# A second copy of the scan state, and its scaled copy made earlier, in an encoder layer

## The chip, the cores and the metric

The kernel runs on one core of a Trainium2 chip. The metric is the device time of one execution in microseconds (us); lower is better. A core has five engines with a queue of instructions each: PE (matmuls, with the loading of weights shown apart as PEld), DVE (elementwise work), ACT (elementwise work and functions), POOL (elementwise work) and SP (here it only issues DMAs). Each engine takes its instructions in the order of the program; between engines they wait on semaphores.

## The reference

One encoder layer over two sequences, of 512 and 1024 tokens, with 1024 features. It has a feed-forward part, then a mixer, then a second feed-forward part. Half of the mixer is a linear recurrence (`wkv_scan`), run forwards and backwards over 8 heads of 64 features:

```python
def step(S, inp):
    r_t, w_t, k_t, v_t, na_t, b_t = inp
    sa = jnp.einsum('bhvk,bhk->bhv', S, na_t)
    S = S * w_t[:, :, None, :] + sa[..., None] * b_t[:, :, None, :] + v_t[..., None] * k_t[:, :, None, :]
    y = jnp.einsum('bhvk,bhk->bhv', S, r_t)
    return S, y
...
m = jnp.concatenate([pool_mixer(...), rwkv7_mixer(...)], axis=-1)
m = m.astype(x.dtype) @ w_out
```

S is a 64 x 64 matrix for each head and direction, zero at the start. All values are float32.

## The kernel before

The kernel works on three blocks of 512 tokens (two of the long sequence, one of the short one). The feed-forward parts and projections are long runs of dense matmuls: 128x128 weights on 512 columns, each product in three matmuls (high x high, high x low, low x high halves of the values; tiles `hh`, `hl`, `gh`, `gl` and weights `whi`, `wlo`). They write PSUM tiles named `u`, `v` and `y`. There are 11556 of them.

The recurrence is computed in chunks of L = 64 tokens. Two heads go together, so there are four pairs of heads for each sequence. A "macro" is 8 chunks (two groups `gi` of 4 chunks `c`), with both directions `d` side by side; 12 macros make 96 chunks. `scan_prep` makes a group's operands (AR, BKt, MU), `scan_inv` inverts its triangular matrices by columns on DVE or POOL, `scan_state` runs through the chunks in order, and `scan_post` normalises the result. The projection `wout_gen` of a block waits for the result of `scan_post`.

A chunk of `scan_state` has three steps, each ended by a `yield WAIT`:

1. **W**: matmuls (lines 1366 and 1369) multiply the old state SBD by AR, and MA by part of UV, into the direction's PSUM bank, columns 0 to 127; ACT copies W to `iw` (line 1371; the profile calls its tile XN).
2. **U**: matmuls (line 1375) into columns 128 to 255 of the bank; ACT copies U into UV (line 1377; the profile calls its tile MU). Then ACT makes `s0p`, the old state scaled by the decay of the chunk (line 1381).
3. **Update and output**: matmuls of line 1386 put the state's increment into columns 0 to 63; lines 1391 (reads the old state) and 1393 put the chunk's output into 64 columns from 256 on. DVE then writes the new state over the old one: increment x decay + `s0p` (lines 1399 and 1401), in four instructions: two directions by two heads.

The last chunk of a pair of heads makes no update, and the first has no old state. The 8 PSUM banks include one for each direction, `bank[d]`, which holds W, U, the increment and the output of four chunks.

The order of all instructions is made while the program is built. `run_until` keeps a set of processes (the dense stream, the four scan processes, norms) and emits the next piece of the ready one with the best priority. Whether one is ready is decided by `Estimate`, a table of costs: it keeps a time at which each engine is free, and for each region of a tile when it was last written and read. After `yield WAIT` the state's process is ready again 200 ns after the estimated end of everything that its step issued; until then dense matmuls are emitted. `Estimate` compares regions of the state's bank by address. The waits themselves are not from this table; they are added afterwards from what each instruction reads and writes.

Of the kernel before, what the change touches and what calls it, by code (L numbers as in the profile page):

```python
# [12 lines left out]
AF = mybir.ActivationFunctionType  # L13
ALU = mybir.AluOpType
# [3 lines left out]
P = 128  # L18
# [5 lines left out]
L = 64  # L24
# [140 lines left out]
def rev(ap):  # L165
    a = [list(x) for x in ap.ap]
    st, n = a[-1]
    a[-1] = [-st, n]
    return bass.AP(tensor=ap.tensor, offset=ap.offset + st * (n - 1), ap=a)
# [3 lines left out]
def encoder_kernel(ctx, tc, x_prompt, x_sample, c_prompt, c_sample, ada_w, ada_b, n1_pre, n1_post,  # L173
# [5 lines left out]
    V, S, G, T, SY = (Queue(est, *q) for q in (("V", nc.vector), ("S", nc.scalar), ("G", nc.gpsimd), ("T", nc.tensor),  # L179
                                               ("Y", nc.sync)))  # L180
# [3 lines left out]
    def nm(s):  # L184
        uid[0] += 1
        return f"{s}{uid[0]}"
# [15 lines left out]
    def mt(shape, tag, bufs, dt=F32, pool=None):  # L202
        return est.ring((pool or mp).tile(shape, dt, name=nm(tag), tag=tag, bufs=bufs), (id(pool), tag), bufs)
# [4 lines left out]
    class Proc:  # L208
        def __init__(self, gen, prio):
            self.gen, self.prio, self.ready, self.cond = gen, prio, est.free["T"], None  # L210
# [67 lines left out]
    def has(*k):  # L278
        return lambda: all(x in flags for x in k)

    def mm(out, lhsT, rhs, start=True, stop=True):
        T.matmul(out, lhsT, rhs, start=start, stop=stop, skip_group_check=True)
# [853 lines left out]
    class ScanBufs:  # L1136
        def __init__(self, sp):
            self.sp = sp
            f = lambda shape, n: sp.tile(shape, F32, name=nm(n), tag=n, bufs=1)
            self.AR = f([P, 2, 2, 4, 2, L], "AR")  # L1140
            self.BKt = f([P, 2, 2, 4, P], "BKt")
            self.MU = f([P, 3, 32, L], "MU")
            self.MA, self.MR = self.MU[:, 0], self.MU[:, 1]
            self.UV = self.MU[:, 2].rearrange("p (g d c h) f -> p g d c h f", g=2, d=2, c=4)
            self.XN = f([P, 61, 32], "XN")
            self.iw = self.XN[0:64, 53:61, :].rearrange("p t s -> p (t s)")
            self.SBD = f([P, 2, P], "SBD")
            self.Pt = f([P, 2, 4, L + 1], "Pt")
            self.PL = f([P, 2, 2, 2, 4], "PL")
            self.bank = [ps.tile([P, TB], F32, name=nm("sb"), tag=f"s{d}", bufs=1) for d in range(2)]  # L1150
            G.memset(self.SBD, 0.0)
            G.memset(self.Pt, 1.0)
            self.yT, self.bq = {}, {}

# [2 lines left out]
    def st_(sb, shape, tag, bufs=1):  # L1157
        return mt(shape, tag, bufs, pool=sb.sp)
# [183 lines left out]
    def scan_state(sb):  # L1342


        AR, BKt, UV, MA, MR, SBD, PL = sb.AR, sb.BKt, sb.UV, sb.MA, sb.MR, sb.SBD, sb.PL
        both = range(2)
        half = [slice(64 * h, 64 * h + 64) for h in both]
        Wp = [sb.bank[d][half[d], 0:P] for d in both]
        Up = [sb.bank[d][half[d], P:2 * P] for d in both]
        hl_ = lambda h: slice(h * L, (h + 1) * L)  # L1350
        for m, (i_, hf) in enumerate(macros):
            g, p = pairs[i_]
            nblk = GT[g] // GL
            nh = nblk // 2
            for c8 in range(8):
                gi, c = c8 // 4, c8 % 4
                if c == 0:
                    yield has(("inv", m, gi))
                zero = hf == 0 and c8 == 0
                lastc = hf == nh - 1 and c8 == 7  # L1360
                us = lambda d, h: gi * 16 + d * 8 + h * 4 + c
                wsb = [sb.iw[:, d * P:(d + 1) * P] for d in both]
                s0p = {}
                if not zero:
                    for d in both:
                        mm(Wp[d], AR[:, gi, d, c, 0, :], SBD[:, d, :], stop=False)
                for h in both:
                    for d in both:
                        mm(Wp[d][:, hl_(h)], MA[64:128, us(d, h), :], UV[64:128, gi, d, c, h, :], start=zero)
                for d in both:  # L1370
                    S.activation(wsb[d], Wp[d], AF.Copy)
                yield WAIT
                for h in both:
                    for d in both:
                        mm(Up[d][:, hl_(h)], MA[0:64, us(d, h), :], wsb[d][:, hl_(h)])
                for d in both:
                    S.activation(UV[0:64, gi, d, c].rearrange("p h f -> p (h f)"), Up[d], AF.Copy)
                if not zero and not lastc:
                    for d in both:
                        s0p[d] = st_(sb, [P, P], f"s0p{d}")  # L1380
                        S.activation(s0p[d], SBD[:, d, :], AF.Copy, scale=PL[:, m % 2, gi, d, c:c + 1])
                yield WAIT
                if not lastc:
                    for d in both:
                        for h in both:
                            mm(sb.bank[d][half[h], 0:L], BKt[:, gi, d, c, half[h]], UV[:, gi, d, c, h, :])
                yo = slice(256 + c * L, 256 + c * L + L)
                for d in both:
                    if not zero:
                        for h in both:  # L1390
                            mm(sb.bank[d][half[h], yo], SBD[half[h], d, half[h]], AR[half[h], gi, d, c, 1, :], stop=False)
                    for h in both:
                        mm(sb.bank[d][half[h], yo], UV[:, gi, d, c, h, :], MR[:, us(d, h), :], start=zero)
                if not lastc:
                    for d in both:
                        for h in both:
                            pl_ = PL[half[h], m % 2, gi, d, c:c + 1]
                            if zero:
                                V.tensor_scalar(SBD[half[h], d, half[h]], sb.bank[d][half[h], 0:L], pl_, None, op0=ALU.mult)
                            else:  # L1400
                                V.scalar_tensor_tensor(SBD[half[h], d, half[h]], sb.bank[d][half[h], 0:L], pl_,
                                                       s0p[d][half[h], half[h]], ALU.mult, ALU.add)
                if c == 3:
                    t = 2 * hf + gi
                    if t == 0:
                        if i_ >= 1:
                            yield has(("post", i_ - 1))
                        sb.yT[i_] = st_(sb, [P, GT[g]], "yT")
                    for d in both:
                        gb = t if d == 0 else nblk - 1 - t  # L1410
                        o = sb.yT[i_][:, gb * GL:(gb + 1) * GL]
                        if d == 1:
                            o = rev(o)
                        if t >= nh:
                            V.tensor_tensor(o, o, sb.bank[d][:, 256:512], ALU.add)
                        else:
                            S.activation(o, sb.bank[d][:, 256:512], AF.Copy)
                        flags.add(("st", m, gi, d))
                yield WAIT
# [183 lines left out]
    with tc.tile_pool(name="late", bufs=1, reuse_waits="tile") as lp:  # L1603
        sb = ScanBufs(lp)
        scanning.append(sb)

        spawn(scan_state(sb), 0)
        spawn(scan_inv(sb, 0), PRIO_INV)
        spawn(scan_inv(sb, 1), PRIO_INV)
        spawn(scan_prep(sb), PRIO_PREP)  # L1610
        spawn(scan_post(sb), PRIO_POST)

        run_until(has(("m", 1), ("m", 0)))
        scanning.clear()
# [35 lines left out]
```

## Time and profile before

| | |
|---|---|
| timed runs, us | 3717.42, 3724.97, 3725.17 (median 3724.97) |
| profiled execution, us | 3731.42, with a span of 3729.7 |
| mean granted clock of PE | 0.948 |
| matmuls into the scan's bank (sb) | first at about 1265 us, last at about 2660 us |
| s0p on ACT | 160 instructions, mean 392 ns |
| writes of the state on DVE | 352 instructions, median 284 ns |

The profile lists instructions by tiles, as out<-in, with buffer numbers left out; x4 behind a row says that four were merged. All instructions carry the line of one helper (L161), so that rows are told apart by their tiles. `sb<-SBD,AR` is the part of W with the old state, `sb<-XN,MU` is U, `sb<-MU,BKt` is the increment, `sb<-AR,SBD` and `sb<-MU` behind it are the output, and `SBD<-sb,PL,s0p` is the update. A value in brackets is the engine's idle time just before the row, with what ended it.

### The profile page before, as it was taken

To read this page: it belongs to the slowest core of one execution; us is meant where nothing else is said; L and a number is where in the kernel's file an instruction comes from. 1 tells how busy PE (TensorE), PEld (TensorE's weight loads), DVE (VectorE), ACT (ScalarE), POOL (GpSimd) and SP (SyncE) were. 2 spreads that over 40 slices of the span, in tenths; PEclk is the share of its full clock that TensorE was granted. 3 is DMA by queue.
4 is the path that set the end of the run, shared out by engine and by line. 5 is a ranking of instruction groups with operands and counts; after the bars stand their busy time and mean duration, and the time that the engine had idled before them with its cause. 6 is when DMAs were issued, how large, how long until landed. Compare 5 with 4: busy or idle time off the path is not lost. (4 is left out here: it accounts for less than half of the span.)

```text
span 3729.7 us, 53665 instructions
## 1 busy us (share of the span) xinstructions
PE 3511.1 (94%) x19579; PEld 2656.5 (71%) x19579; DVE 2014.5 (54%) x3817; ACT 1443.7 (39%) x2778; POOL 1399.6 (38%) x1700
## 2 busy tenths in 40 slices
PE   7999999998999999999889978899999999999998
PEld 4667878886676676776656656667787788877886
DVE  3128262227227878787877687777557522242223
ACT  3324252224335444444444434444334432233222
POOL 2333444443232322233414324432354344444444
PEclk8999999998999998999979978799999999999999
DMA  7655343334344322222423343222354333334332
GB/s 277 226 183 180 92 150 99 90 99 122 123 123 141 91 66 89 74 83 83 138 79 105 111 147 119 69 85 64 99 181 130 111 109 90 100 117 121 95 92 79
DMA packets 557980, 432.11 MB, mean 116 GB/s; under 512 B 27029, under 2 KB 511572, under 8 KB 553620
## 3 DMA queue, kind: packets, MB, share of 16 engines
q1 hardware_dynamic: 524900, 379.90, 33.2%
q10 hardware_dynamic: 32816, 48.78, 4.1%
q8 instruction: 155, 2.54, 0.3%
q14 instruction: 109, 0.89, 0.1%
HBM read 367.23 MB, written 61.34 MB: 115 GB/s over the span
## 5 line engine op out<-in xcount | busy, mean ns | idle before, releaser
L161 POOL TENSOR_TENSOR wlo<-wraw,whi 128x512 fp32r<-128x512 f32 x666 | 884.9, 1347 | 1288.3 <-ACT whi L161 819.6
L161 DVE TENSOR_TENSOR y<-y,y 128x512 f32<-128x512 f32 x480 | 328.1, 685 | 879.9 <-PE y L161 878.8
L161 ACT ACTIVATE whi<-wraw 128x512 fp32r<-128x512 f32 x938 | 559.4, 622 | 184.8 <-PE v L161 141.3
L161 PE MATMUL u<-hl,whi 128*128 128x512 f32 x1392 | 568.4, 408 | 19.5 <-DVE hl L161 18.4
L161 PE MATMUL u<-hh,whi 128*128 128x512 f32 x1392 | 568.9, 409 | 15.8 <-ACT hh L161 4.2
L161 PE MATMUL v<-hh,whi 128*128 128x512 f32 x1392 | 566.5, 407 | 11.6 <-ACT hh L161 6.2
L161 PE MATMUL v<-hl,whi 128*128 128x512 f32 x1392 | 565.9, 407 | 8.3 <-DVE hl L161 8.3
L161 PE MATMUL u<-hh,wlo 128*128 128x512 f32 x1392 | 570.7, 410 | 0.1
L161 PE MATMUL v<-hh,wlo 128*128 128x512 f32 x1392 | 565.1, 406 | 0.0
L161 PE MATMUL y<-gh,whi 128*128 128x512 f32 x1056 | 424.8, 402 | 9.9 <-DVE y L161 8.2
L161 PE MATMUL y<-gh,wlo 128*128 128x512 f32 x1056 | 423.8, 401 | 2.5 <-DVE wlo L161 2.5
L161 PE MATMUL y<-gl,whi 128*128 128x512 f32 x1056 | 422.4, 400 | 0.0
L161 POOL TENSOR_TENSOR XN<-XN 64x126 f32<-64x126 f32 (+22 forms) x744 | 331.2, 445 | 177.3 <-DVE XN L161 60.7
L161 ACT ACTIVATE gh<-s 128x512 fp32r<-128x512 f32 x132 | 83.5, 632 | 644.9 <-DVE s L161 644.9
L161 PEld LDWEIGHTS u<-hl,whi 128*128 128x128 f32 x1392 | 268.3, 193 | 88.7 <-DVE hl L161 24.8
L161 PEld LDWEIGHTS u<-hh,whi 128*128 128x128 f32 x1392 | 268.6, 193 | 86.5 <-ACT hh L161 7.9
L161 PEld LDWEIGHTS v<-hh,whi 128*128 128x128 f32 x1392 | 266.9, 192 | 80.7 <-ACT hh L161 9.7
L161 PEld LDWEIGHTS v<-hl,whi 128*128 128x128 f32 x1392 | 267.0, 192 | 75.7 <-DVE hl L161 12.5
L161 PEld LDWEIGHTS u<-hh,wlo 128*128 128x128 f32 x1392 | 268.4, 193 | 70.2 <-issue 10.2
L161 PEld LDWEIGHTS v<-hh,wlo 128*128 128x128 f32 x1392 | 267.4, 192 | 64.7 <-issue 7.2
L161 PEld LDWEIGHTS y<-gh,whi 128*128 128x128 f32 x1056 | 200.5, 190 | 63.9 <-DVE y L161 11.6
L161 PEld LDWEIGHTS y<-gh,wlo 128*128 128x128 f32 x1056 | 200.8, 190 | 51.3 <-DVE wlo L161 3.7
(252 smaller groups left out, 4322.6 us busy)
## 6 DMA issues: line engine op xcount, KB each, us to landing
wraw<-in_f_w_dram SPq DMA_DIRECT2D x792, 256.0 KB
ada<-in_ada_w_dram SPq DMA_DIRECT2D x32, 1024.0 KB
wraw<-in_w_in_dram SPq DMA_DIRECT2D x98, 256.0 KB
xk<-xs ACTq DMA_DIRECT2D x96, 256.0 KB
xs<-y ACTq DMA_DIRECT2D x48, 256.0 KB
wraw<-in_w_out_dram SPq DMA_DIRECT2D x48, 256.0 KB
in_k<-zk SPq DMA_DIRECT2D x48, 128.0 KB
in_kk<-zkk SPq DMA_DIRECT2D x48, 128.0 KB
```

Source lines behind the costliest of these rows:

```text
L161: return f(*args, **kw)
```

## The change

There are two copies of the state, and chunks take turns: chunk `c8` reads copy `c8 % 2` and writes the other. Both are set to zero once, since only their diagonal blocks are written later. And `s0p` is made in step 1, after the copies of W, instead of in step 2, after the copies of U.

```diff
-            self.SBD = f([P, 2, P], "SBD")
+            self.SBD = [f([P, 2, P], "SBD%d" % i) for i in range(2)]
...
-            G.memset(self.SBD, 0.0)
+            for t in self.SBD:
+                G.memset(t, 0.0)
...
+                old, new = SBD[c8 % 2], SBD[1 - c8 % 2]
                 if not zero:
                     for d in both:
-                        mm(Wp[d], AR[:, gi, d, c, 0, :], SBD[:, d, :], stop=False)
+                        mm(Wp[d], AR[:, gi, d, c, 0, :], old[:, d, :], stop=False)
...
                 for d in both:
                     S.activation(wsb[d], Wp[d], AF.Copy)
+                if not zero and not lastc:
+                    for d in both:
+                        s0p[d] = st_(sb, [P, P], f"s0p{d}")
+                        S.activation(s0p[d], old[:, d, :], AF.Copy, scale=PL[:, m % 2, gi, d, c:c + 1])
                 yield WAIT
...
                 for d in both:
                     S.activation(UV[0:64, gi, d, c].rearrange("p h f -> p (h f)"), Up[d], AF.Copy)
-                if not zero and not lastc:
-                    for d in both:
-                        s0p[d] = st_(sb, [P, P], f"s0p{d}")
-                        S.activation(s0p[d], SBD[:, d, :], AF.Copy, scale=PL[:, m % 2, gi, d, c:c + 1])
                 yield WAIT
...
-                            mm(sb.bank[d][half[h], yo], SBD[half[h], d, half[h]], AR[half[h], gi, d, c, 1, :], stop=False)
+                            mm(sb.bank[d][half[h], yo], old[half[h], d, half[h]], AR[half[h], gi, d, c, 1, :], stop=False)
...
-                                V.scalar_tensor_tensor(SBD[half[h], d, half[h]], sb.bank[d][half[h], 0:L], pl_,
+                                V.scalar_tensor_tensor(new[half[h], d, half[h]], sb.bank[d][half[h], 0:L], pl_,
                                                        s0p[d][half[h], half[h]], ALU.mult, ALU.add)
```

Line 1399, the update of a first chunk, changes in the same way. Since `Estimate` sees other tiles and another order on ACT, the order of the whole program behind the scan's start changes. Three places show how. The numbers behind the names only tell buffers apart.

On ACT, one chunk of the second macro before: the copies of W (XN), then of U (MU), then s0p for both directions.

```order
L161 ACTIVATE XN_9076<-sb_9080 64x128
L161 ACTIVATE XN_9076<-sb_9081 64x128
L161 ACTIVATE MU_9075<-sb_9080 64x128
L161 ACTIVATE MU_9075<-sb_9081 64x128
L161 ACTIVATE s0p_11118<-SBD_9077,PL_9079 128x128
L161 ACTIVATE s0p_11120<-SBD_9077,PL_9079 128x128
```

The same chunk on ACT now:

```order
L161 ACTIVATE XN_9076<-sb_9081 64x128
L161 ACTIVATE XN_9076<-sb_9082 64x128
L161 ACTIVATE s0p_11109<-SBD_9078,PL_9080 128x128
L161 ACTIVATE s0p_11111<-SBD_9078,PL_9080 128x128
L161 ACTIVATE MU_9075<-sb_9081 64x128
L161 ACTIVATE MU_9075<-sb_9082 64x128
```

The two s0p instructions moved ahead of the copies of U, and read the copy of the state whose turn it is.

On PE, in the same macro, from the last matmul of W to the first of U, before (rows with 128x512 are dense matmuls):

```order
L161 MATMUL sb_9081<-MU_9075 64x64
L161 MATMUL u_10964<-hl_8857,whi_10885 128x512
L161 MATMUL u_10964<-hh_8856,wlo_10960 128x512
L161 MATMUL y_11109<-gh_10417,whi_10871 128x512
L161 MATMUL y_11109<-gl_10418,whi_10871 128x512
L161 MATMUL sb_9080<-XN_9076,MU_9075 64x64
```

And the same piece of PE now:

```order
L161 MATMUL sb_9082<-MU_9075 64x64
L161 MATMUL u_10966<-hl_8857,whi_10887 128x512
L161 MATMUL u_10966<-hh_8856,wlo_10962 128x512
L161 MATMUL y_11121<-gh_10423,whi_10873 128x512
L161 MATMUL y_11121<-gl_10424,whi_10873 128x512
L161 MATMUL y_11121<-gh_10423,wlo_10889 128x512
L161 MATMUL y_11121<-gh_10689,whi_10873 128x512
L161 MATMUL y_11121<-gl_10690,whi_10873 128x512
L161 MATMUL y_11121<-gh_10689,wlo_10889 128x512
L161 MATMUL sb_9081<-XN_9076,MU_9075 64x64
```

Four more dense matmuls stand between W and U; in the same chunk four fewer, 4 for 8, stand between U and the increment.

On PE, from that chunk's output to the W of the next chunk, before:

```order
L161 MATMUL sb_9081<-AR_9073,SBD_9077 64x64 x2
L161 MATMUL sb_9081<-MU_9075 64x64 x2
L161 MATMUL v_11140<-hl_8729,whi_10958 128x512
L161 MATMUL v_11140<-hh_8728,wlo_11003 128x512
L161 MATMUL v_11140<-hh_8728,whi_10958 128x512
L161 MATMUL sb_9080<-SBD_9077,AR_9073 64x128
```

And now:

```order
L161 MATMUL sb_9082<-AR_9073,SBD_9078 64x64 x2
L161 MATMUL sb_9082<-MU_9075 64x64 x2
L161 MATMUL v_11148<-hl_8729,whi_10960 128x512
L161 MATMUL v_11148<-hh_8728,wlo_11005 128x512
L161 MATMUL sb_9081<-SBD_9077,AR_9073 64x128
```

One dense matmul fewer stands ahead of the matmul that needs the new state.

More of the change, by code (lines that the diff above doesn't have):

```diff
@@ L1398, in scan_state @@
                             if zero:
-                                V.tensor_scalar(SBD[half[h], d, half[h]], sb.bank[d][half[h], 0:L], pl_, None, op0=ALU.mult)
+                                V.tensor_scalar(new[half[h], d, half[h]], sb.bank[d][half[h], 0:L], pl_, None, op0=ALU.mult)
                             else:
-                                V.scalar_tensor_tensor(SBD[half[h], d, half[h]], sb.bank[d][half[h], 0:L], pl_,
+                                V.scalar_tensor_tensor(new[half[h], d, half[h]], sb.bank[d][half[h], 0:L], pl_,
                                                        s0p[d][half[h], half[h]], ALU.mult, ALU.add)
```

## The prediction

> **What bounds the kernel now.** I read the page first, for the engine that is always busy.
>
> ```profile
> span 3729.7 us, 53665 instructions
> ...
> PE 3511.1 (94%) x19579; PEld 2656.5 (71%) x19579; DVE 2014.5 (54%) x3817; ACT 1443.7 (39%) x2778; POOL 1399.6 (38%) x1700
> ```
>
> PE is busy for 94% of the span. Its instructions are the same before and after, so the time can change only through PE's idle time and the clock that is granted to it. The change acts only while the scan runs, roughly from 1265 to 2660 us. Second, therefore, the windows of that part: length, PE busy, weight loads, DVE, ACT, POOL, then the granted clock and DMA.
>
> ```profile
> 1300.00:1600.00 300.00, 289.87 (x2268) 208.82 (x2268) 230.39 (x532) 129.15 (x292) 72.67 (x146) 0.93 0.26 78
> 1600.00:1900.00 300.00, 270.89 (x2059) 194.55 (x2057) 246.44 (x520) 140.14 (x304) 126.00 (x223) 0.90 0.32 97
> 1900.00:2200.00 300.00, 271.08 (x1943) 191.57 (x1944) 222.98 (x529) 138.61 (x306) 89.04 (x192) 0.86 0.35 105
> 2200.00:2500.00 300.00, 262.90 (x1933) 187.87 (x1932) 228.74 (x496) 132.63 (x293) 115.46 (x196) 0.82 0.33 102
> ```
>
> In these 1200 us PE idles 105.3 us (1200 less the four busy times), and its clock is 0.93 falling to 0.82. Third, PE's waits between 1174 and 2662 us: total, times, longest.
>
> ```profile
> PE sM L161 <- DVE MU L161: 35.8, 23, 4.1
> PE sb L161 <- DVE SBD L161: 17.0, 26, 2.2
> ...
> PE sb L161 <- ACT MU L161: 3.6, 3, 1.8
> ...
> PE sb L161 <- ACT XN L161: 2.9, 4, 1.0
> ```
>
> The largest wait belongs to the triangular inverse, which is not edited. The three waits of the chunk chain are W (old state, SBD), U (copy of W, named XN) and the update (copy of U, named MU): 17.0 + 2.9 + 3.6 = 23.5 us in all. That is the most that a perfect chunk chain could return directly.
>
> **The change part by part.**
>
> *Two copies of the state.* The stated dependency is that DVE may not overwrite SBD until line 1391 has read it; with two copies only the matmuls of line 1386 are ahead of the write. One covered chunk, on PE and then on DVE, shows whether that read is what DVE waits for.
>
> ```profile
> 1500.57 0.45 PE L161 MATMUL sb<-MU,BKt 128*64 128x64 f32 x8
> 1500.96 0.33 PE L161 MATMUL sb<-AR,SBD 64*64 64x64 f32 x4
> 1501.22 0.34 PE L161 MATMUL sb<-MU 128*64 128x64 f32 x4
> 1501.48 0.33 PE L161 MATMUL sb<-AR,SBD 64*64 64x64 f32 x4
> 1501.74 0.34 PE L161 MATMUL sb<-MU 128*64 128x64 f32 x4
> 1502.01 0.50 PE L161 MATMUL v<-hh,whi 128*128 128x512 f32 x1
> ```
> ```profile
> 1500.63 0.84 DVE L161 TENSOR_TENSOR wlo<-wraw,whi 128x512 fp32r<-128x512 f32 x1
> 1501.67 0.58 DVE L161 SCALAR_TENSOR_TENSOR SBD<-sb,PL,s0p 64x64 f32<-64x64 f32 x2 [0.20 <-PE sb L161]
> ```
>
> DVE is free at 1501.47 (1500.63 + 0.84). The reads of the old state for the first direction ended at 1501.29 (1500.96 + 0.33). Yet DVE idles 0.20 us more, and starts only after the next row's end, 1501.56 (1501.22 + 0.34). That row is line 1393: it writes other columns of the same PSUM bank and touches nothing that the update reads or writes. The same shows where no value is shared at all, on ACT's copy of the outputs (yT, columns 256 to 511):
>
> ```profile
> ACT yT L161 <- DVE SBD L161: 11.8, 15, 3.7
> ```
>
> Fifteen times ACT waited for the update, which reads columns 0 to 63. The order is kept per bank, not per column. In the built programs the first write of each direction waits for the count of line 1393's last matmul in that direction's bank, in all 88 chunks that update, in both kernels. So the wait that the second copy would remove has a twin that stays, and I cost the direct gain at 0 us. [...]
>
> The planner does not know of the bank. Its estimate now lets the update start after line 1386, so it places the next W earlier than DVE can deliver. Of 95 gaps between a chunk's last output matmul and the next W, 6 held two rows or fewer before and 16 do now. What a row is worth there:
>
> ```profile
> 1384.83 1.23 DVE L161 SCALAR_TENSOR_TENSOR SBD<-sb,PL,s0p 64x64 f32<-64x64 f32 x4 [0.62 <-issue]
> ```
> ```profile
> 1386.07 0.47 PE L161 MATMUL sb<-SBD,AR 128*64 128x128 f32 x4
> 1386.47 0.45 PE L161 MATMUL sb<-MU 64*64 64x64 f32 x8
> 1386.85 0.50 PE L161 MATMUL v<-hl,whi 128*128 128x512 f32 x1
> ...
> 1387.97 0.45 PE L161 MATMUL sb<-XN,MU 64*64 64x64 f32 x8
> ```
>
> With three rows the update ended at 1386.06 and W began at 1386.07: nothing to spare. From 1386.85 to U at 1387.97 four dense rows take 1.12 us, 0.28 us each. One row fewer costs at most that, and nothing where W's first half needs only the first direction. Ten gaps give 0 to 2.8 us, **+1.5** taken, about the middle. If all 26 late states lost a row, it would be 26 x 0.28 = 7 us: the upper end.
>
> *The scaled copy s0p moves between the copies of W and of U on ACT.*
>
> ```profile
> 1387.00 0.57 ACT L161 ACTIVATE XN<-sb 64x128 f32<-64x128 f32 x2 [1.62 <-PE sb L161]
> 1388.45 0.57 ACT L161 ACTIVATE MU<-sb 64x128 f32<-64x128 f32 x2 [0.88 <-PE sb L161]
> 1388.92 0.69 ACT L161 ACTIVATE s0p<-SBD,PL 128x128 f32<-128x128 f32 x2
> ```
>
> It is 0.69 us for both directions, and ACT has 0.88 us of idle time just there. The planner makes room: between W and U the usual count of dense matmuls goes from 4 to 8 (48 chunks before, 43 now), and between U and the update from 8 to 4 (48 and 43). The cover is exchanged. Four rows were enough before U: copies end at 1387.57, U starts at 1387.97; the copies of U take the same 0.57. So the waits of 2.9 and 3.6 us exchange places: **0**, between -2.9 and +2.9. If two ACT copies of weights stood between, that cover would be gone and the wait for MU would return at its present 1.8 us each. The update's own wait for s0p goes, but no view shows it as the last to arrive.
>
> *One more memset.*
>
> ```profile
> L161 POOL MEMSET SBD<- 128x256 f32 x1 | 0.3, 312 | 0.0
> ```
>
> 0.3 us on POOL, once, ahead of the scan's first loads: 0.
>
> *The moved stage switch.* The planner's order shifts against the dense stream. The scan's last matmul now stands after 7250 dense ones instead of 7281. At dense row 6420, where the output projection waits for its first tile, 36 other matmuls stood between two dense rows; now 94 do, with two whole chunks without any cover. What a stretch like it costs is in the trace, first the switch itself, then a later stretch with uncovered chunks (columns as above):
>
> ```profile
> 2215.00:2228.00 13.00, 7.60 (x74) 5.60 (x73) 5.86 (x11) 4.23 (x9) 1.11 (x1) 0.61 0.97 315
> 2325.00:2350.00 25.00, 19.55 (x184) 15.53 (x184) 17.07 (x45) 8.45 (x19) 4.64 (x3) 0.55 0.25 79
> ```
> ```profile
> 2327.73 1.32 PE L161 MATMUL sb<-SBD,AR 128*64 128x128 f32 x4 [1.59 <-DVE SBD L161]
> ...
> 2332.57 1.91 PE L161 MATMUL sM<-MU 32*32 32x32 f32 x32 [1.55 <-DVE MU L161]
> ...
> 2337.19 0.48 PE L161 MATMUL sb<-MU 128*64 128x64 f32 x4
> ```
>
> An uncovered chunk lasted from 2327.73 to 2337.67, less the 1.91 us of the inverse: 8.0 us. A covered one costs PE 0.78 (1386.07 to 1386.85) + 0.45 + 1.44 (1500.57 to 1502.01) = 2.7 us. Two uncovered ones cost 10.6 us more. Against that the switch already idles 5.4 us (13.00 - 7.60), which the two chunks can fill: between -5.4 and +10.6. The nearest row, 2325 to 2350, has 5.45 us idle with such chunks inside, as much as the switch has without; the middle is **+2.5**, and I take it.
>
> **Sum:** 0 + 1.5 + 0 + 0 + 2.5 = +4 us, 0.1%. The profiled execution took 3731.42 us (span 3729.7, 1.7 around it), which becomes 3735; it lies 6.4 us above the timed median of 3724.97, and the same +4 on the median gives **3729 us**.
>
> **The rivals.**
>
> *Slower: the uncovered chunks hold up the output projection.* PE takes its rows in order, so the dense rows wait behind both chunks even when their tile is there. It decides once the two chunks last longer than the 13 us of the switch. The price: 10.6 + 1.5, and 8 us more at a clock near the 0.55 of the row above, worth 4: +16, 3741 us. For it: 16 us (twice 8.0) is more than 13. Against: part of the 8.0 us is half clock that the switch has already (0.61). [...]
>
> *Faster: the new order is kinder to the clock.* Over the 1200 us above the mean clock is 0.878; one hundredth more is worth 1200 x 0.01 / 0.878 = 13.7 us, so -14 + 0 gives 3711 us. For it: the scan ends 31 dense rows earlier. Against: the same small matmuls run, and the shifts have no direction. The same hundredth downward adds to the case above.
>
> *Faster: the update does start by address.* Then it starts 0.65 us earlier (1501.67 against 1501.02, where line 1386's rows end) and the 17.0 us of waits go: 3708 us. Against it stand the 0.20 us and ACT's 11.8 us above.
>
> **How the numbers follow.** About 0.2% (7.4 us) is what a measurement of this kernel can tell from no change. Forecast 0.42, of which 0.32 lies within 0.2% and 0.10 above it (its upper ends); slower rival 0.27; kinder clock 0.22, of which 0.03 stays within; by address 0.06; a remaining 0.03 within. Faster 0.19 + 0.06 = 0.25, same 0.38, slower 0.37. The range reaches from 3704 (the address case less its spread) to 3753 (the slower rival with a hundredth of clock on top, less 2 for the part already counted). The forecast alone would be 3720 to 3740.
>
> **What would show it.** Right: DVE's SBD rows still start after the second group of output matmuls, not at line 1386's end; PE's wait for SBD goes up from 17.0 us to 18 to 24; those for XN and MU exchange their sizes; the s0p rows stand between the XN and MU rows; clock within 0.01 in the four windows. Wrong: SBD rows that start 0.65 us earlier; a wait for SBD under 10 us; a stretch around the output projection's start that is over 10 us longer; or a clock that moved by over a hundredth, which would outweigh every term of the sum.

## The result, and the profile after

The changed kernel takes 3698.17 us (median of four runs, 3696.6 to 3699.62), against 3721.6 us (3717.42 to 3725.17) for the kernel before in the same comparison: a ratio of 0.9932, with an interval of 0.9915 to 0.995. It is faster by 23 us, 0.7%. The forecast was 3729 us, and the range began at 3704 us: the prediction was wrong, in its sign and in its range.

The profiled execution took 3696.6 us, 34.8 us less than the one of before (3731.42). That one lies 10 us above the median of its kernel, so what two profiles differ by is more than the 23 us. The page of after, with the span and then the busy time of each engine:

```profile
span 3694.9 us, 53680 instructions
...
PE 3489.5 (94%) x19579; PEld 2639.9 (71%) x19579; DVE 2009.6 (54%) x3813; ACT 1436.3 (39%) x2776; POOL 1408.9 (38%) x1705
```

PE has the same 19579 instructions, and is busy for 21.6 us less (3511.1 before). Work that is the same and takes less busy time points at the clock, not at waits. The four windows of the scan follow: length, busy time of PE, weight loads, DVE, ACT, POOL, then granted clock and DMA.

```profile
1300.00:1600.00 300.00, 291.05 (x2324) 208.80 (x2324) 240.88 (x546) 134.55 (x303) 86.25 (x174) 0.96 0.27 80
1600.00:1900.00 300.00, 267.74 (x2027) 190.67 (x2021) 244.23 (x524) 136.70 (x301) 116.65 (x198) 0.90 0.32 96
1900.00:2200.00 300.00, 277.43 (x2004) 195.57 (x2004) 230.26 (x548) 136.65 (x302) 94.30 (x190) 0.90 0.38 114
2200.00:2500.00 300.00, 268.91 (x2101) 192.75 (x2102) 236.00 (x504) 143.74 (x319) 124.73 (x222) 0.85 0.33 101
```

The clock was 0.93, 0.90, 0.86, 0.82 and is now 0.96, 0.90, 0.90, 0.85: three windows of four gained three to four hundredths, and none lost. All runs on record say the same: over the whole execution the clock was 0.955 to 0.958 in the four runs of after (mean 0.9565), and 0.947 to 0.955 (mean 0.951) in the 22 runs of before that stand beside e1 to e4. PE's idle time here fell from 105.3 to 94.9 us. PE's waits between 1174 and 2662 us, as total, times and longest:

```profile
PE sM L161 <- DVE MU L161: 37.1, 23, 4.2
PE sb L161 <- DVE SBD L161: 18.6, 32, 2.2
...
PE sb L161 <- ACT XN L161: 1.9, 4, 1.0
...
PE sb L161 <- ACT MU L161: 0.8, 2, 0.5
```

The chunk chain's waits were 17.0 + 2.9 + 3.6 = 23.5 us and are 18.6 + 1.9 + 0.8 = 21.3 us. The chain that the change edits gave 2 us; the kernel gained 23.

Most of the idle time that went lay elsewhere: in waits of the dense matmuls themselves for `hl`, the low half of the values, which DVE makes. In the same stretch, before:

```profile
PE u L161 <- DVE hl L161: 15.7, 7, 3.7
PE v L161 <- DVE hl L161: 7.1, 2, 3.8
```

After, where `v` has no such wait any more:

```profile
PE u L161 <- DVE hl L161: 11.3, 7, 3.2
```

That is 22.8 us before and 11.3 after. The edit touches none of these instructions, only the order around them.

**Where along the program the time went.** PE runs the same dense matmuls in the same order in both kernels, so the start of the n-th one can be compared (worked out from both traces, after less before). Counted here are PE's rows of 512 columns into `u`, `v` or `y`: 11592, 36 more than the 11556 dense matmuls by which the prediction counts, since the 36 in float32 stand as two rows each, 72 in the trace. Single values depend by up to 4 us on where the count stands:

| dense matmul | 4550 | 4700 | 5600 | 6350 | 6500 | 6800 | 7100 | 7400 |
|---|---|---|---|---|---|---|---|---|
| difference, us | -0.4 | -4.4 | -12 | -19 | -11 | -25 | -33 | -34.6 |

Before the scan and behind it the two run alike. The gain is spread over all of the scan, with one loss, at the stage switch between 6350 and 6500. Summed over the trace, PE's gaps went from 206.4 to 193.0 us, and the clock records' time at one half from 391.0 to 318.6 us (some 2 us of each lie behind the last instruction).

### The profile page after: what moved, and what is told of

Read it like the earlier page. It is cut to its first block, busy times and chain, and to the rows that moved or that the text cites. A ratio compares the mean times of both kernels' runs of the same rounds, so it can differ in the third digit from the quotient of the medians.

```text
span 3694.9 us, 53680 instructions
## 1 busy us (share of the span) xinstructions
PE 3489.5 (94%) x19579; PEld 2639.9 (71%) x19579; DVE 2009.6 (54%) x3813; ACT 1436.3 (39%) x2776; POOL 1408.9 (38%) x1705
## 5 line engine op out<-in xcount | busy, mean ns | idle before, releaser
L161 PE MATMUL y<-gh,whi 128*128 128x512 f32 x1056 | 425.5, 403 | 12.3 <-DVE y L161 11.3
```

Of the source, the lines that this page charges most:

```text
L161: return f(*args, **kw)
```

## The experiments

Times are medians; the ratio is to the kernel before in the same comparison, with its interval.

| run | what it is | us | ratio | interval |
|---|---|---|---|---|
| e1_two_only | two copies, s0p in its old place | 3718.22 | 0.9998 | 0.9982 to 1.0014 |
| e2_s0p_only | one copy, s0p moved | 3735.28 | 1.0046 | 1.0024 to 1.0068 |
| e3_two_old_order | two copies, order of before | 3721.57 | 0.9999 | 0.9982 to 1.0015 |
| e4_one_new_order | one copy, order of after | 3703.38 | 0.9952 | 0.9935 to 0.9969 |
| e5_by_bank | after, planner counts banks as wholes | 3717.81 | 0.9985 | 0.9971 to 1.0 |

### Each half of the change alone

For e1 the four lines of s0p go back behind the copies of U, and the rest is as after:

```diff
-                if not zero and not lastc:
-                    for d in both:
-                        s0p[d] = st_(sb, [P, P], f"s0p{d}")
-                        S.activation(s0p[d], old[:, d, :], AF.Copy, scale=PL[:, m % 2, gi, d, c:c + 1])
                 yield WAIT
...
+                if not zero and not lastc:
+                    for d in both:
+                        s0p[d] = st_(sb, [P, P], f"s0p{d}")
+                        S.activation(s0p[d], old[:, d, :], AF.Copy, scale=PL[:, m % 2, gi, d, c:c + 1])
                 yield WAIT
```

> Two copies of the state, s0p made after the copies of U as before. If the gain comes from where the planner now puts W (it counts the update as ready earlier), most of the 23 us are here: 3695 to 3710 us. If it comes from the exchanged cover around U, nothing is here: 3715 to 3727 us.

For e2 the state has one copy again, and s0p stays in its new place:

```diff
-            self.SBD = [f([P, 2, P], "SBD%d" % i) for i in range(2)]
+            self.SBD = f([P, 2, P], "SBD")
...
-                        S.activation(s0p[d], old[:, d, :], AF.Copy, scale=PL[:, m % 2, gi, d, c:c + 1])
+                        S.activation(s0p[d], SBD[:, d, :], AF.Copy, scale=PL[:, m % 2, gi, d, c:c + 1])
```

> One copy of the state, s0p made after the copies of W. If the gain comes from the exchanged cover around U (8 dense matmuls ahead of U and 4 behind it), most of the 23 us are here: 3695 to 3710 us. If it comes from the second copy or from where W now stands, nothing is here: 3715 to 3727 us.

e1 changed nothing (0.9998), and e2 made the kernel slower by 0.46%, some 17 us. Together the two edits give -23 us: the parts don't add. Neither place by itself is the gain. In e1 W does stand earlier: of the 88 gaps from an output to the next W that reads an old state, the trace shows two rows or fewer in 16 (15 after, 4 before). In e2 eight dense matmuls stand between W and U in 40 chunks (43 after). The windows of e2, columns as above:

```profile
1300.00:1600.00 300.00, 290.28 (x2224) 209.55 (x2222) 233.01 (x531) 128.03 (x289) 73.32 (x146) 0.91 0.27 80
1600.00:1900.00 300.00, 272.12 (x2108) 195.42 (x2107) 233.04 (x498) 130.44 (x295) 120.28 (x219) 0.91 0.31 96
1900.00:2200.00 300.00, 271.40 (x1894) 189.16 (x1895) 235.78 (x557) 138.08 (x304) 94.27 (x196) 0.83 0.33 100
2200.00:2500.00 300.00, 266.76 (x1949) 189.87 (x1948) 223.71 (x486) 138.45 (x305) 114.40 (x191) 0.80 0.33 103
```

PE idles 99.4 us here (1200 less the four), less than before's 105.3, and waited 13.4 us for SBD in the scan (17.0 before). By waits e2 should have been faster. The clock is what went the other way: 0.91, 0.91, 0.83 and 0.80. This profile is the slowest of e2's six runs (3750.97 us), but the mean clock of all six, 0.947, lies below the 0.951 of before too.

### The copies without the order, the order without the copies

Both edits act on two things: on the waits that are put into the program, and on the order that the planner makes. The next two kernels part them. In e3 the chip has two copies and the planner takes them for one, so that the order is that of before, row for row on PE, DVE, ACT and SP:

```diff
-        name = ap.tensor.name
+        name = self.alias.get(ap.tensor.name, ap.tensor.name)
...
+            est.alias[self.SBD[1].tensor.name] = self.SBD[0].tensor.name
+            G.memset(self.SBD[0], 0.0)
+            nc.gpsimd.memset(self.SBD[1], 0.0)
```

> Two copies of the state on the chip, but the planner counts them as one tile and s0p stays in its old place, so that PE, DVE, ACT and SP have the old order row for row. If the second copy does nothing on the chip because the bank keeps the wait: 3717 to 3726 us, as before, with the update starting 0.2 us before the start of the last output matmul. If the second copy works on the chip: 3695 to 3705 us.

In e4 the planner sees two copies, and every instruction gets the first one, so that the order is that of after on all engines:

```diff
+    def real(self, x):
+        if hasattr(x, "tensor") and hasattr(x, "offset") and x.tensor.name in self.one:
+            t = self.one[x.tensor.name]
+            return bass.AP(tensor=t, offset=x.offset, ap=[list(q) for q in x.ap])
+        return x
...
+            args = [self.est.real(x) for x in args]
+            return f(*args, **{k: self.est.real(x) for k, x in kw.items()})
...
+            est.one[self.SBD[1].tensor.name] = self.SBD[0].tensor
```

> One copy of the state on the chip, but the planner counts two and s0p is moved, so that every engine has the new order row for row. If the gain is a matter of order alone: 3695 to 3702 us, as the changed kernel. If the second copy works on the chip: 3715 us or more.

e3, with the copies, is worth nothing (0.9999), and e4, with the order alone, takes 3703.38 us, a little above the range given for order alone. That is 18 of the 23 us, with an interval that overlaps that of after. What the copies were to bring, a shorter wait for the state, didn't come: 17.0 us before, and in e3 and in e4 (total, times, longest):

```profile
PE sb L162 <- DVE SBD L162: 17.8, 28, 2.2
```
```profile
PE sb L171 <- DVE SBD L171: 18.5, 33, 2.2
```

The waits for `hl` go with the order too: 21.6 us in e3 and 12.0 us in e4, in the same stretch (22.8 before, 11.3 after).

So the gain is that of the order: 18 of the 23 us by the medians. For the second copy alone no gain is measured (e3, -0.18% to +0.15%). The 5 us between e4 and after are within the two intervals; whether the copy adds a little in the new order, these runs don't settle.

### Other orders of the same two programs

If the order alone is worth -23 us in one case and +17 us in another, how far do orders scatter? Twelve kernels change one constant of the planner by a little, some in the program of before and some in that of after; the instructions are the same, and only their order moves:

```diff
-AFTER_STATE = 200
+AFTER_STATE = 205
```
```diff
-CHAIN_LEAD = 300
+CHAIN_LEAD = 310
```

The number in a label is the constant's new value: AFTER_STATE for 190, 205, 220 and 230, CHAIN_LEAD for 310 and 320, AFTER_OTHER (400) for 410; "pipe" has PIPE_LEAD at -310 (-300).

> The kernel before, with the planner's pause after a step of the scan at 205 instead of 200 ns: no work changes, only the order. If the gain is a draw among orders, such an edit moves the time by 5 to 25 us either way. If the time follows the chain of a chunk, it stays within 4 us of before.

> The changed kernel, with the same pause at 205 instead of 200 ns. If the gain is a draw among orders, the 23 us don't hold: anywhere from 3690 to 3735 us. If the new arrangement (8 dense matmuls ahead of U, 4 behind, W earlier) is what gains, it stays at 3694 to 3704 us.

> The kernel before, with the planner's lead for the steps of the inverse at 310 instead of 300 ns: order alone. Draw among orders: 5 to 25 us either way. Otherwise within 4 us of before.

> The changed kernel, with the lead for the steps of the inverse at 310 instead of 300 ns. Draw among orders: 3690 to 3735 us. If the new arrangement gains: 3694 to 3704 us.

> The changed kernel with the pause after a step at 220 instead of 200 ns, another order. Draw among orders: 3695 to 3740 us, with no tie to the changed kernel's 3698. If the new arrangement gains and the one miss (lead 310) was chance: 3694 to 3708 us.

> The changed kernel with the pause at 190 instead of 200 ns, another order again. Draw among orders: 3695 to 3740 us. If the new arrangement gains: 3694 to 3708 us.

> The kernel before with the lead for the inverse's steps at 320 instead of 300 ns, another order. Draw among orders: 3695 to 3745 us, at times as fast as the changed kernel. If the old arrangement is the slower one: 3715 us or more.

> The kernel before with the pause at 220 instead of 200 ns. Pure draw among orders: 3700 to 3745 us, below before as often as above. New arrangement faster on average: 3720 us or more, as the other old orders.

> The kernel before with the pause of the other scan processes at 410 instead of 400 ns. Pure draw: 3700 to 3745 us. New arrangement faster on average: 3720 us or more.

> The changed kernel with the lead for the norms at -310 instead of -300 ns. Pure draw: 3700 to 3745 us. New arrangement faster on average: 3695 to 3725 us.

> The changed kernel with the pause at 230 instead of 200 ns. Pure draw: 3700 to 3745 us. New arrangement faster on average: 3695 to 3725 us.

> The kernel before with the pause at 230 instead of 200 ns. Pure draw among orders: 3700 to 3745 us. New arrangement faster on average: 3720 us or more.

And the kernel of after whose planner counts the two banks as wholes, as the waits in the program do:

```diff
+            est.whole.update(b.tensor.name for b in self.bank)
```

> The changed kernel, with a planner that counts each of the scan's two banks as a whole, as the chip's waits do: W stands later again. If W's earlier place (one row fewer) carries the gain, it goes: 3715 to 3727 us. If better-placed work gains further: under 3695 us. If the time is a draw among orders: anywhere from 3690 to 3740 us.

| program | run: us, ratio, interval |
|---|---|
| of before | 205: 3739.46, 1.0042 (1.0024 to 1.0061); 220: 3727.22, 1.0007 (0.9989 to 1.0026); 230: 3714.97, 0.9982 (0.9965 to 0.9998); 320: 3728.92, 1.0006 (0.9991 to 1.002); 410: 3722.01, 0.9987 (0.9971 to 1.0004); 310, which came out in the order of before: 3719.37, 0.9991 (0.9972 to 1.001) |
| of after | 205: 3697.7, 0.9925 (0.9897 to 0.9954); 220: 3707.11, 0.9954 (0.9937 to 0.9971); 190: 3733.91, 1.0019 (1.0005 to 1.0034); 230: 3719.72, 0.9985 (0.9968 to 1.0003); 310: 3722.25, 0.9992 (0.9977 to 1.0007); pipe: 3713.65, 0.9971 (0.9958 to 0.9985) |

An order that is repeated repeats its time to about 0.2%: e3 and p_before_310 that of before; e4 and p_after_205, in which only 73 rows on PE stand elsewhere than after, that of after (0.9932, 0.9952, 0.9925). Another order of the same instructions gives anything from -0.7% to +0.4%. The six different orders of the old arrangement lie at +0.04% on the mean, the six of the new one (after itself among them, and p_after_205 left out as a repeat) at -0.25%. The difference of 0.29%, some 11 us, has a standard error of 0.15%: the new arrangement may be better on the mean, but these draws don't settle it, the more so as after is the order that the question began with: without before and after themselves the means are +0.05% and -0.16%. Nor does it hold the gain from order to order: 190 and 310 of after took 3733.91 and 3722.25 us, where the new arrangement was to give at most 3708 and 3704, and 230 of before took 3714.97, where the old one was to give 3720 or more. e5's planner, which knows the bank, is no better either: 3717.81 us, with two rows or fewer in 2 of the 88 gaps. That fits a draw, and it fits W's earlier place as the gain; against the latter stands e1.

### What halves the clock

Over the 19 profiles up to here the span goes with PE's idle time (correlation 0.77), and more closely with the time at half clock (0.94). Their records have the clock at 1 or at one half, and it changes only on a grid of 3.413 us (76 records before and 54 after, every edge on the grid to 0.003 us). The grid's first edge lies between 8.3 and 11.4 us from the start of the span in these profiles. Steps at half clock during the scan: 88 before, 68 after, 105 in e2, 69 in e4. The steps at half clock came mostly after steps in which the matmuls had streamed few columns; how long PE had idled in them sorted them worse (455 steps sorted wrongly against 1464, with the counts at the end of this section). Few columns and idle time go together in this program, so the last run parts them. It adds stretches of matmuls behind the end of the changed kernel:

```diff
+        full(200)
+        for _ in range(200):
+            mm(pq[:, 0:P], ident, ident)
+        full(200)
+        for _ in range(600):
+            mm(pq[0:32, 0:32], ident[0:32, 0:32], ident[0:32, 0:32])
+        full(200)
+        groups(25, 8, 1)
+        full(200)
+        groups(25, 8, 2)
+        full(200)
+        groups(40, 2, 1)
+        full(100)
```

Here `full(n)` is n dense matmuls, and `groups(n, k, copies)` n times k dense ones with that number of copies on ACT, the last of which the next group waits for.

> The changed kernel with stretches of matmuls on zeros and the identity added behind its end; no output reads them, and the time as a whole isn't compared. Question: what sends PE's clock to one half. Work theory, from 19 profiles: the clock is set on a grid of 3.413 us, and is halved after a step in which the matmuls streamed fewer than about 3000 columns (sum of the last number of their form), idle or not; whole again after a step with more. Wait theory: it is halved by PE's idle time. Stretches, between runs of 200 dense matmuls (128x512): (1) 200 matmuls of 128x128 in float32 without a gap, 0.213 us each, 2050 columns in a step; (2) 600 of 32x32 without a gap, 0.035 to 0.06 us each, 1800 to 3100 columns; (3) 25 groups of 8 dense ones, each followed by a copy on ACT that the next waits for, a gap of about 1 us, 4900 columns; (4) the same with two copies, a gap of about 1.6 us, PE idle nearly half the time, 4000 columns; (5) 40 groups of 2 dense ones with one copy, 2400 columns. Work theory: (1) half but for the first two steps, clock 0.50 to 0.58; (2) half for most of it; (3) and (4) 1.00, at most one half step; (5) 0.50 to 0.60. Wait theory: (1) and (2) 1.00, as PE has no idle time; (4) worst, (3) and (5) alike. [...]

The five stretches in windows (no other engine but ACT works here), and rows of the second to the fifth on PE:

```profile
3743.00:3788.00 45.00, 45.00 (x404) 44.92 (x402) 0.00 (x0) 0.00 (x0) 0.00 (x0) 1.00 0.00 1
3833.50:3893.50 60.00, 60.00 (x1201) 59.97 (x1200) 0.00 (x0) 0.00 (x0) 0.00 (x0) 0.55 0.01 2
3941.00:4012.00 71.00, 52.46 (x201) 35.39 (x199) 0.00 (x0) 14.57 (x25) 0.00 (x0) 1.00 0.00 0
4058.00:4141.00 83.00, 52.42 (x201) 35.38 (x199) 0.00 (x0) 26.96 (x50) 0.00 (x0) 1.00 0.00 0
4187.00:4264.00 77.00, 46.87 (x80) 19.03 (x78) 0.00 (x0) 23.89 (x40) 0.00 (x0) 0.53 0.00 0
```
```profile
3844.80 2.42 PE L161 MATMUL u<-ident 32*32 32x32 f32 x42
...
3946.47 0.50 PE L161 MATMUL u<-qx,qw 128*128 128x512 f32 x1 [0.75 <-ACT qx L161]
...
4071.05 0.50 PE L161 MATMUL u<-qx,qw 128*128 128x512 f32 x1 [1.24 <-ACT qx L161]
...
4200.82 0.79 PE L161 MATMUL u<-qx,qw 128*128 128x512 f32 x1 [0.75 <-ACT qx L161]
```

The second stretch has no idle time in its rows (60.00 of 60.00 us busy), and runs at 0.55. The fourth waits 1.24 us before each of its groups, idles for 37% of its time (52.42 of 83.00 us busy), and runs at 1.00. The third and the fifth have the same wait of 0.75 us, and run at 1.00 and at 0.53: the one has 8 dense matmuls between waits, the other 2. The work theory holds for these four. The wait theory falls on the second and the fourth: no wait and 0.55, the longest wait and 1.00. The third and the fifth alone would not decide, since PE idles for a larger share of the fifth: while the clock was still whole, a group started every 1.48 us there, with 0.75 us of it idle.

One thing the trace can't show. The ends of PE's rows are modelled: a 32x32 row is drawn 0.19 to 0.24 us long, while one starts every 0.03 (whole clock) to 0.05 us. How much the array rests inside such rows stays unseen. The stretch excludes waiting between rows as the cause of its 0.55, not an array that is used little, which is what the work theory says in other words. Whether the values play a part (zeros and the identity here) was not tried.

The first stretch was to be at half clock, and ran at 1.00. The expectation there rested on a wrong count: the window shows 404 rows for 200 matmuls, so each float32 matmul is two rows of 0.11 us (45.00 / 404), and a step of 3.413 us streams 128 columns thirty times, 3900, not 2050. That is above the bound of about 3000, so with the right count both theories have whole clock there, and this stretch doesn't decide between them.

With that, all 20 profiles were sorted again: of 21830 steps, 2085 at half clock, a bound on the idle time of the step before sorts 1464 wrongly at best, a bound on its columns 455 (at 3111), and a bound on columns weighted by their form's share of 128x128, the largest form in the traces, those of the small float32 matmuls counted twice, 254 (at about 3000; dense matmuls without a gap, one in 0.23 us, make 7600 in a step). The counts shift by some tens with the way in which a matmul across an edge is shared out. Each of these weightings is a fit, and whether any of them is what sets the clock was not shown. In the second and the fourth stretch the clock followed how much work a step held, and not whether PE waited: 0.55 without idle time, 1.00 with 37% of it.

## Why the prediction was wrong

**Two copies of the state: 0 us.** Right, and shown: e3 has them and is at 0.9999, e4 is without them and keeps 18 of the 23 us. The update still starts after the output's first group. One covered chunk of after, on PE and on DVE:

```profile
1390.50 0.45 PE L161 MATMUL sb<-MU,BKt 128*64 128x64 f32 x8
1390.88 0.33 PE L161 MATMUL sb<-AR,SBD 64*64 64x64 f32 x4
1391.14 0.34 PE L161 MATMUL sb<-MU 128*64 128x64 f32 x4
1391.40 0.33 PE L161 MATMUL sb<-AR,SBD 64*64 64x64 f32 x4
```
```profile
1391.58 1.18 DVE L161 SCALAR_TENSOR_TENSOR SBD<-sb,PL,s0p 64x64 f32<-64x64 f32 x4 [3.95 <-issue]
```

DVE had idled for 3.95 us; the profile names no releaser for it ("issue"), but the times tell. The increment was there at 1390.95 (1390.50 + 0.45), and the old state is now in the other copy. DVE starts at 1391.58, 0.10 us after the first direction's output row, which shares only the bank, ends (1391.14 + 0.34 = 1391.48). It is so throughout: in each of the traces of before, after, e3 and e4, none of the 88 updates starts before that row's end plus 0.05 us, and of the 80 whose chunk has an old state, 26 to 32 start within 0.2 us of it. So in these four programs the update stays behind a row with which it shares the bank and no address. The rival "by address" is excluded.

**W earlier by a row: +1.5 us.** The wait for SBD went from 17.0 to 18.6 us, inside the predicted 18 to 24: +1.6. Profiles of one order differ by as much: 17.0, 17.8 and 15.5 us in before, e3 and p_before_310; 18.6, 18.5 and 19.3 in after, e4 and p_after_205. Most of the short gaps cost nothing: in 12 of the 15 with two rows or fewer PE doesn't wait, and the other three make 1.9 us. W's first half needs only the first direction, as the prediction allowed. In this one W starts before the update ends:

```profile
1384.92 1.23 DVE L161 SCALAR_TENSOR_TENSOR SBD<-sb,PL,s0p 64x64 f32<-64x64 f32 x4 [4.70 <-issue]
```
```profile
1385.94 0.70 PE L161 MATMUL sb<-SBD,AR 128*64 128x128 f32 x4
```

**s0p between the copies: 0 us.** The rows stand as predicted:

```profile
1387.10 0.57 ACT L161 ACTIVATE XN<-sb 64x128 f32<-64x128 f32 x2 [3.19 <-PE sb L161]
1387.57 0.68 ACT L161 ACTIVATE s0p<-SBD,PL 128x128 f32<-128x128 f32 x2
1389.47 0.57 ACT L161 ACTIVATE MU<-sb 64x128 f32<-64x128 f32 x2 [1.22 <-PE sb L161]
```

The exchange of cover shows in the weight loads' waits (before, then after), which fell for XN from 21.8 to 6.5 us and rose for MU from 6.5 to 13.8 us:

```profile
PEld sb L161 <- ACT XN L161: 21.8, 51, 1.4
...
PEld sb L161 <- ACT MU L161: 6.5, 9, 2.2
```
```profile
PEld sb L161 <- ACT MU L161: 13.8, 34, 0.7
...
PEld sb L161 <- ACT XN L161: 6.5, 13, 1.2
```

On PE itself they didn't exchange, as the prediction had it: both fell, 2.9 to 1.9 and 3.6 to 0.8 us, -3.8 in all, a little past its bound of -2.9.

**The stage switch: +2.5 us.** It lost time, as predicted, but at the upper bound and not at the middle (-5.4 to +10.6 were given): 7.9 us from row 6350 to row 6500 of the table, and 11.0 us between the two dense matmuls right around it, before and after:

```profile
2214.69 0.39 PE L161 MATMUL u<-hh,wlo 128*128 128x512 f32 x1
...
2227.91 0.80 PE L161 MATMUL u<-hh,whi 128*128 128x512 f32 x1 [1.20 <-ACT hh L161]
```
```profile
2194.95 0.39 PE L161 MATMUL u<-hh,wlo 128*128 128x512 f32 x1
...
2212.32 1.32 PE L161 MATMUL sb<-SBD,AR 128*64 128x128 f32 x4 [0.54 <-DVE SBD L161]
...
2216.55 0.78 PE L161 MATMUL sb<-MU,BKt 128*64 128x64 f32 x8 [0.52 <-ACT MU L161]
...
2219.21 0.79 PE L161 MATMUL u<-hh,whi 128*128 128x512 f32 x1 [0.23 <-ACT hh L161]
```

13.2 us became 24.3 us, 11.0 longer, so the line "a stretch around the output projection's start that is over 10 us longer", which was to show the forecast wrong, did come true. The two chunks were to fill the 5.4 us that PE idles here, and didn't: by the windows of these two stretches PE idles 5.4 us before and 6.0 us after, and its busy time grows from 7.8 to 18.3 us. Part of that is only moved, since chunks that the old order ran elsewhere are inside, with short waits (0.54 and 0.52 us here). The row for an uncovered chunk, 8.0 us, was also that of a pair's last chunk: it has no increment and no update.

**The step that failed: the price of the new order.** The prediction costed the reorder at the two places where it could see a mechanism, +1.5 and +2.5, and put everything else at nothing, with the reason that "the shifts have no direction". As a rival beside the sum it allowed a hundredth of the clock either way, 13.7 us, with a chance of 0.22 for the kinder side. Two terms that the sum left out turned out to be the largest.

- The clock. The mean of the scan's four windows rose by 0.025 (0.878 to 0.903), two and a half times the hundredth allowed; in e2 it fell by 0.015. A straight-line fit over the 19 profiles (span = 3412 us + 0.97 x idle + 0.31 x time at half clock) gives it 22 of the 34.8 us between the profiles (72.4 x 0.31).
- The idle time outside the chunk chain. The sum had +4 us for waits and uncovered chunks; PE's gaps fell by 13.4 us, which the fit makes 13 us. The waits of dense matmuls for `hl`, 11.5 us less in the scan, are the largest part, and no term of the prediction has them.

The medians differ by 23 us and not by 34.8. From the mean clocks of all runs, 0.951 and 0.9565, the time at half clock is estimated at 364 and 322 us, and by the fit its 42 us are worth 13 of the 23; the other 10 are left for idle time. By the same fit a hundredth of the clock over the scan's 1200 us, 24 us more or less at half clock, is worth 7.4 us and not 13.7. So the rival had the direction right, its hundredths too few and the price of each too high. The split is a fit, not an experiment; that most of the gain belongs to the order is what e3 and e4 show.

So the sum was made of the small terms. Of its four local ones, those of the chunk chain came out within a few us, the switch at its upper bound, and none of them is the gain, while what no row of before could price was larger than all of them. The trace of before did hold a hint: the prediction quoted a stretch at 0.55 of the clock with PE busy for 19.55 of 25 us, and used it only for the 4 us in the price of its slower rival. Read on, it holds only small matmuls, without a dense one between them (PE's rows from 2325 to 2350), and suggests that they went with the 0.55 though PE was busy, and that an order which thins them out with dense matmuls may have fewer steps at half clock. The scatter of orders measured above has a standard deviation of 0.21% and 0.30%, 8 and 11 us, for clock and idle time together. With that as the spread of the whole sum, the range down to 3704 us was 1.6 of the larger deviation below the 3721.6 us of before, and 3698 us is 2.1 of it. That this order came out so far on the good side, no row of before could tell: it is a far draw, or the new arrangement is better on the mean, as said above.

Why this order has fewer steps with little work, is not settled. By the weighted count above, about 90 steps of the scan are below 3000 columns before, 71 to 75 after, 78 in e4 and 105 in e2. That is the same fact at a finer grain, since no run moved chosen rows. The version that is fastest is the changed kernel as it stands; p_after_205 equals it, and no run beat it.

## What to carry to other kernels

When an edit makes a planner or a scheduler lay out the whole program anew, the layout is a term of its own: price it by the scatter of a few orders of the same instructions, and part it from the edit by a kernel that has the one without the other, as e3 and e4 do. A gain of half a per cent from one such order doesn't show that the edit is good. Where stretches of small matmuls lie beside dense ones, look at the granted clock step by step, even where PE never waits: 0.55 here in the stretch of 32x32 matmuls without idle time. Spreading the small ones so that no 3.4 us are left with little work is the edit that follows from it; no run here has tried it by itself.

## What the runs showed of the hardware

- In these profiles the granted clock was recorded as 1 or one half, and changed on a grid of 3.413 us. In two stretches of e6 it followed the work and not the wait: without a gap between their rows, 32x32 matmuls ran at 0.55; with 1.24 us of waiting before each group of 8 dense ones the clock stayed at 1.00. Over 20 profiles a bound on the idle time of the step before sorted 1464 of 21830 steps wrongly, a bound on its columns 455.
- At whole clock a float32 matmul of 128 columns stood as two rows of 0.11 us (e6, 404 rows for 200 matmuls in 45.00 us), a dense one of 512 columns as one of 0.23 us (before and after, from start to start without a gap).
- The update of the state started no earlier than 0.05 us after the end of the first direction's output row, with which it shares only the PSUM bank, in all 88 chunks of before, after, e3 and e4.
- The grid's place against the program was not the same in all profiles: its first edge lies between 8.3 and 11.4 us (at 9.33 us in before and in after). One order had 88 half steps in the scan in one profile and 78 in another (before, and p_before_310), with spans of 3729.7 and 3715.1 us. Whether that grid is the whole of the spread between runs of one kernel, was not tried.
